# Block sums laid in one run, block products in another order, and down units split by adding DMAs in a two-layer encoder

## The chip, the cores and the metric

The kernel runs on one core of one Trainium2 chip. The metric is the device time of one execution in microseconds (us); the times given are medians of several runs. The engines are named as in the profile: PE is TensorE (matmuls), PEld its weight loads, DVE is VectorE, ACT is ScalarE, POOL is GpSimd, and SP is the engine that issues most of the DMAs.

## What is computed

The reference is an encoder of two layers on 512 frames of 1024 features, in float32. Each layer has a half-weighted feed-forward block (FFN), a mixer and another FFN:

```python
for layer in range(DEPTH):                       # DEPTH = 2
    h = _rmsnorm(x, ffn1_norm[layer])
    x = x + 0.5 * _swiglu(h, ffn1_w_gate[layer], ffn1_w_up[layer], ffn1_w_down[layer])
    h = _rmsnorm(x, mix_norm[layer])
    ...                                          # even: SSD and S5 mixers; odd: band attention and pooling
    x = x + mixed
    h = _rmsnorm(x, ffn2_norm[layer])
    x = x + 0.5 * _swiglu(h, ffn2_w_gate[layer], ffn2_w_up[layer], ffn2_w_down[layer])

def _swiglu(h, w_gate, w_up, w_down):            # 1024 -> 2816 -> 1024
    return (jax.nn.silu(h @ w_gate) * (h @ w_up)) @ w_down
```

The four FFNs hold most of the work: 3 x 1024 x 2816 weights each. They are numbered 0 to 3 (`f0` to `f3`); the even mixer lies between `f0` and `f1`, the odd one between `f2` and `f3`.

## The kernel before

**Products in three parts.** The kernel multiplies in `float32r`, a rounded form of float32. So that little precision is lost, each operand is split in a high part (a rounded copy) and a low part (what the copy left over), and each product is three matmuls: high x high, high x low, low x high (`mm3`, L596). A tile `whl` of [128, 2, 1024] holds both parts of 128 x 1024 weights, a tile `hg` of [128, 2, 512] both parts of an activation.

**Units.** Weights come in units of 128 x 1024 (512 KB). `load_raw` (L498) issues the load into a `raw` tile from SP. The feeder (`feed`, L508) then splits the unit in one of two ways. `split` (L565) has ScalarE write the rounded copy and VectorE subtract it from the raw weights. `split_dma` (L576) has ScalarE write the negative of the rounded copy into the low part, lets a DMA from POOL's queue add the weights to it from HBM, and has ScalarE write the high part: no VectorE, one more ScalarE copy and a second reading of the weights. `BY_DMA` (L52) says which units go which way: the key is the unit's name with, for `wgu` and `wdn`, the FFN's number; the range is over the unit's index (`by_dma`, L105). For `wdn` that index is the half of the output columns, `cg`, which is 0 or 1.

**FFN items.** `ffn_items` (L69) lists an FFN's work: 11 pairs of hidden tiles (q = 0 to 10), each with a gate (i = 0) and an up side (i = 1). The first q (eight in FFN 0, two in FFNs 1 to 3) are done in the plain way, four units `wgu` of 24 matmuls with 512 columns per q. The rest are "pairs". The down units (`wdn`, 22 in an FFN, 24 matmuls with 512 columns each) of a group of three q are put between the items of the next group, so that in the steady part a pair and a down unit take turns.

**Pairs.** A pair multiplies a 2 x 2 arrangement of weight blocks by a 2 x 2 arrangement of activation blocks with seven block products in place of eight. Sums of weight blocks (made by VectorE from two raw units, L541 to L551) and sums of activation blocks (`blocks`, L876, once per FFN) go into it. W1 and W2 are blocks of the weights themselves, W3 and W4 hold sums; N are the normed activations; TA and TB are lists of four `hg` tiles with sums, each of two sums of 256 columns. `block` (L904) is one block product of four steps: three matmuls of 256 columns in each, or, where it is `wide`, one of 512 columns (high weights by the high and the low part of a block sum at once) and one of 256. The parts of a block sum lie 512 elements apart, so that a wide matmul reads two runs of 256.

`pair` (L924) works in three PSUM banks X, Y and Z. In the order of the code before, with the names that are used below:

| block | line | what |
|---|---|---|
| X1 | L940 | W1 x N[0:4] into X; VectorE then makes p1 from it |
| Z4 | L944 | W4 x N[4:8] into one half of Z |
| (rest) | L946 | the last block of an earlier pair, where no down unit came between |
| Y3 | L949 | W3 x TA into Y, wide; `plus` then reads both halves of Y (two additions) |
| X1b | L951 | W1 x N[4:8], added to X |
| Z3 | L955 | W3 x TA into the other half of Z |
| Y4 | L962 | W4 x TB, wide, added to Y; `plus` reads Y again |
| Y2 | L969 | W2 x TB, wide, added to Y, after the next down unit |

An addition to a bank that VectorE has yet to read has to wait for that reading. Y2 takes its weights from the smaller tile `wh`, so its matmuls show as `ps<-hg,wh`; all other blocks and the down units show as `ps<-hg,whl`. Only q = 2, i = 1 of FFNs 1 to 3 has an earlier pair's rest in front of it (`before` in the code); the other 57 of 60 pairs do not.

**The order of the work** is written out by the program itself. `Clock` (L111) is a model of the engines and DMAs with a cost for each operation. At every few matmuls, `tick` (L285) lets the feeder and the waiting threads put in what the model holds to be ready (`on`, L320: the inputs are there, and the engine's queue is short enough). Threads stand in the order of `PRIO` (L58): a lower number goes first; among equal ones, a new thread goes in front, except `evac` (the reading of a plain unit's PSUM), which goes behind. While the FFN 0 runs, the thread `prep` prepares the S5 mixer with many small VectorE operations. All the program's instructions are issued through one helper, so that the profile gives L207 for them; groups are told apart by their tiles.

Of the kernel before, what the change touches and what calls it, by code (L numbers as in the profile page):

```python
# [14 lines left out]
PSUM = bass.MemoryType.PSUM  # L15
# [17 lines left out]
for _i, _pools in enumerate(((),(3,),(2,),(1,0))):  # L33
# [18 lines left out]
BY_DMA = {"wgu1": (1, 4), "wgu2": (1, 4), "wgu3": (1, 4), "wev": (13, 16), "wglu": (0, 2), "wevo": (0, 1), "wod": (8, 16), "wodo": (0, 1)}  # L52
# [5 lines left out]
PRIO = {"evac": 0, "gate": 0, "small": 5, "prep": 6, "blocks": 0, "s5_bounce": 1, "s5_quarter": 0, "s5_gate": 0, "s5_eighth": 1,  # L58
        "ssd_dt": 1, "conv": 1, "ssd_chunk": 1, "ssd_tail": 0, "z": 2, "qk_norm": 0, "pool": 3, "attn": 2}
LIVE = 3  # L60
CHAINS = 2
# [49 lines left out]
class Clock:  # L111


    def __init__(self):
        self.t = dict.fromkeys(list(ENGINES.values()) + ["RING", "DMA"], 0.0)
        self.t["ACT"], self.t["RING"], self.t["DVE"], self.t["PE"] = 1.9, 0.65, 0.6, 0.95
        self.w, self.r, self.floor, self.stuck = {}, {}, 0.0, 0
        self.lanes, self.born = [0.0] * 8, {}

    @property  # L120
# [24 lines left out]
    def cost(eng, op, out, kw):  # L145
# [12 lines left out]
        ptr = any(hasattr(kw.get(k), "space") for k in ("scalar", "scalar1"))  # L158
        return (0.128 if ptr else 0.068) + n / (1920 if one else 960) * (1 if eng == "DVE" else 2)

    def note(self, eng, op, args, kw):
        out = kw.get("out", args[0] if args else None)
        outs = [out] + ([kw["accum_out"]] if "accum_out" in kw else [])
        ins = [v for k, v in kw.items() if k not in ("out", "accum_out") and hasattr(v, "free_size")]
        dma = op == "dma_start"
        at = self.t["RING"] if dma else self.t[eng]
        for ap in ins:
            for b in self.blocks(ap):
                t, e = self.w.get(b, (0.0, ""))
                at = max(at, t + (0.15 if e != eng else 0.11 if eng != "PE" else 0.0))  # L170
        for ap in outs:
            at = max(at, self.born.get(ap.name, 0.0))
            for b in self.blocks(ap):
                t, e = self.w.get(b, (0.0, ""))
                at = max(at, 0.0 if dma and e == "DMA" else t if e == eng else t + 0.1, self.r.get(b, 0.0))
        if dma and eng == "POOL":
            self.t["POOL"] = max(at, self.t["POOL"]) + 1.1
            end = max(self.t["DMA"], self.t["POOL"] + 1.0) + max(0.18, out.free_size() * out.partition_size() * 4 / 360e3)
            self.t["DMA"] = end
            end += 0.95  # L180
        elif dma:
            at = max(at, self.lanes.pop(0))
            self.t["RING"] = at + 0.48
            end = max(self.t["DMA"], at + 1.1) + max(0.06, out.free_size() * out.partition_size() * 4 / 360e3)
            self.t["DMA"] = end
            end += 1.06
            self.lanes.append(end)
        else:
            end = at + self.cost(eng, op, out, kw)
            self.t[eng] = end  # L190
        for ap in outs:
            for b in self.blocks(ap):
                self.w[b] = (max(end, self.w.get(b, (0.0, ""))[0]), "DMA" if dma else eng)
        for ap in ins:
            for b in self.blocks(ap):
                self.r[b] = max(self.r.get(b, 0.0), end)
# [55 lines left out]
class Builder:  # L252
# [26 lines left out]

    def phase(self, name):  # L280
        self.name = name
        self.backlog, self.guard, self.most = BACKLOG[name], GUARD[name], AHEAD[name]


# [296 lines left out]

    def split_steps(self, src, dst, scale=None):
        nc = self.nc
        yield from self.on("ACT", src)
        if scale is None:
            nc.scalar.copy(out=dst[:, 0], in_=src)
        else:
            nc.scalar.activation(out=dst[:, 0], in_=src, func=AF.Copy, scale=scale)
        yield from self.on("DVE", dst[:, 0])
        if scale is None:  # L590
            nc.vector.tensor_tensor(out=dst[:, 1], in0=src, in1=dst[:, 0].bitcast(F32), op=ALU.subtract)
        else:
            nc.vector.scalar_tensor_tensor(out=dst[:, 1], in0=src, scalar=scale, in1=dst[:, 0].bitcast(F32),
                                           op0=ALU.mult, op1=ALU.subtract)
# [153 lines left out]
    def ffn(self, f, gi, then, prepare=None):  # L748
        nc, tc = self.nc, self.tc
        self.phase(f"f{f}")  # L750
        self.f, self.then, self.final, self.sideb = f, then, False, 2
        h = self.begin_norm(gi)
        with ExitStack() as st:
            self.ft = st.enter_context(tc.tile_pool(name=self.n("ft"), bufs=2))
            ex = ExitStack()
            prep = None
            if prepare is not None:
                prep = prepare(ex.enter_context(tc.tile_pool(name=self.n("prep"), bufs=1)))
# [11 lines left out]
            self.N, self.TA, self.TB = h, [], []  # L770
            grown, pending = False, None
            for key in ffn_items(f):
                if not grown and not self.running(prep) and CLASSIC[f == 0] < NFF // 2:
# [27 lines left out]
                elif key[0] == "pair":  # L801
                    q, i = key[2:]
                    if i == 0:
                        t = {}
                    last = self.pair(w, t, "us" if i else "gs", pending)

                    def pending(last=last, t=t, q=q, i=i):
                        last()
                        if i == 0:
                            nc.scalar.activation(out=t["gs"], in_=t["gs"], func=AF.Silu)  # L810
                        else:
                            self.add("gate", self.gate(t, g, q, [1] * 4, 1))
                            if q == NFF // 2 - 1:
                                self.give(*self.N, *self.TA, *self.TB)
                else:
                    cg, kp = key[2:]
                    grp = next(gr for gr in GROUPS if kp in gr)
                    if kp == grp[0]:
                        pss = [None] * 4
                        if cg == 0 and grp == GROUPS[-1]:  # L820
                            self.tail()
                    self.out_unit(pss, w, g, kp, cg, kp == grp[0], kp == grp[-1], 0.5, "a")
                    self.give(w)
                    if cg == 1:
                        self.give(g[2 * kp], g[2 * kp + 1])
                    if pending:
                        pending()
                        pending = None
# [47 lines left out]
    def blocks(self, h, gi, late):  # L876
# [5 lines left out]
        for kk in range(4):  # L882
# [11 lines left out]
            v.tensor_tensor(out=t4, in0=n2[:, a], in1=t2, op=ALU.subtract)  # L894
            self.give(tn)
            for c, d in ((lo, self.TA), (hi, self.TB)):
                t = yield from self.grab("hg")
                yield from self.split_steps(rt[:, c], t)
                d.append(t)
            self.give(rt)  # L900
        self.xhold, self.reserve = False, 0


    def block(self, ps, t, at, rhs, c, more=False, wide=False):  # L904
        nc = self.nc
        for kk in range(4):
            self.until(lambda: len(rhs) > kk)
            w = slice(at + kk * P, at + kk * P + P)
            r = rhs[kk]
            first, last = kk == 0 and not more, kk == 3  # L910
            o = ps[:, 0:256]
            go = dict(start=first, stop=False, skip_group_check=more)
            if wide:
                nc.tensor.matmul(out=ps.rearrange("p (a b) -> p a b", a=2), lhsT=t[:, 0, w], rhs=r[:, :, c], **go)
            else:
                nc.tensor.matmul(out=o, lhsT=t[:, 0, w], rhs=r[:, 0, c], **go)
                go["start"] = False
                nc.tensor.matmul(out=o, lhsT=t[:, 0, w], rhs=r[:, 1, c], **go)
            nc.tensor.matmul(out=o, lhsT=t[:, 1, w], rhs=r[:, 0, c], start=False, stop=last, skip_group_check=more)
            self.tick()  # L920


# [1 line left out]
    def pair(self, w, t, tag, before):  # L924
# [26 lines left out]
        self.block(X, W1, 512, N[4:8], lo, more=True)  # L951
        self.give(W1)
        times(dst[:, 0, lo], X[:, lo], lo)
        self.free(X)
# [12 lines left out]

        def last():
            self.block(Y, W2, 0, TB, hi, more=True, wide=wide)  # L969
            self.give(W2)  # L970
            plus(dst[:, 1, lo], Y, p1)
            self.free(Y)
# [1120 lines left out]
```

## Time and profile before

| | |
|---|---|
| runs before | 1817.4, 1820.8, 1824.5 us; median 1820.8 us |
| profiled execution, its own time | 1818.1 us |
| its span, first to last instruction | 1816.4 us |
| granted TensorE clock | 0.999 |
| FFN 0 with what lies beside it | 0 to 367 us: PE busy 360.7, DVE 311.4, ACT 129.7 |
| even mixer | 367 to 545 us: PE 169.2, DVE 150.4, ACT 93.6 |
| FFN 1 | 545 to 932 us: PE 384.5, DVE 326.3, ACT 156.0 |
| FFN 2 | 932 to 1282 us: PE 347.8, DVE 307.6, ACT 137.4 |
| odd mixer | 1282 to 1475 us: PE 192.7, DVE 130.4, ACT 107.7 |
| FFN 3 | 1475 to 1816 us: PE 335.3, DVE 292.6, ACT 122.0 |
| DMA queues | q1 (issued by SP): 196.5 MB; q0 (issued by POOL): 18.4 MB |

In a row that groups instructions stand: line, engine, operation, tiles (out<-in), shape and count; then busy time and the mean length of one in ns; then the engine's idle time just before them and what ended it. A row of waits reads "who waits <- for whom: us in total, times, longest". A row of the timeline has the start, the length from the first start to the last end, and what ran, with the idle time before it in brackets. Lengths of matmuls overlap, since one starts before the one ahead of it has ended: the distance of two starts tells what a matmul costs. A row by stages has the stretch and its length, busy us and number for PE, PEld, DVE, ACT and POOL, the granted clock, the DMA share and GB/s.

### The profile page before, as it was taken

What the parts mean: (1) busy time and instruction counts of PE and PEld (TensorE: products, weight loads), DVE (VectorE), ACT (ScalarE), POOL (GpSimd) and SP (SyncE); (2) the same over time, 40 slices, a digit from 0 to 9 for tenths busy, and PEclk for the clock granted to TensorE, in tenths of its full rate; (3) what the DMA queues carried; (4) which work ended last, traced back from release to release, by engine and by line L of the source; (5) the groups of instructions that cost most, each with busy time, mean ns of one, the idle gap of its engine ahead of it and who ended that gap; (6) DMA issues with size and microseconds to landing.
All of it is one profiled execution on the core that took longest, in us unless ns stands there. A gap on an engine that the chain in (4) does not pass through costs nothing.

```text
span 1816.4 us, 26183 instructions
## 1 busy us (share of the span) xinstructions
PE 1790.0 (99%) x10082; PEld 1535.7 (85%) x10082; DVE 1518.7 (84%) x2902; ACT 746.4 (41%) x1032; POOL 34.0 (2%) x53
## 2 busy tenths in 40 slices
PE   9999999999999999999999999999999999999999
PEld 7877888878778888888888898988888888988887
DVE  8999878777885899998779998987678679999984
ACT  4224433233584533333354333323466564333331
POOL 0000000000010000000010000000000010000000
PEclk9999999999999999999999999999999999999999
DMA  5256433336674532333343333333325452333331
GB/s 194 88 152 194 130 93 93 116 136 196 173 181 139 127 107 96 101 104 107 126 119 102 105 105 105 105 106 115 111 82 116 129 134 87 105 105 104 106 103 71
DMA packets 83341, 216.57 MB, mean 119 GB/s; under 512 B 18288, under 2 KB 30608, under 8 KB 82064
## 3 DMA queue, kind: packets, MB, share of 16 engines
q1 hardware_dynamic: 78032, 196.52, 33.7%
q0 software_dynamic: 5040, 18.35, 6.0%
q8 instruction: 79, 1.29, 0.3%
q14 instruction: 46, 0.38, 0.1%
q10 hardware_dynamic: 144, 0.02, 0.0%
HBM read 202.26 MB, written 12.60 MB: 118 GB/s over the span
## 4 chain that ended last, share of the span: by engine, by line
PE 64%; DVE 23%; DMA 6%; issue 4%; ACT 3%; SPq 0%; DVEq 0%; ACTq 0%
PE ps L207 64%; DVE whl L207 5%; DVE raw L207 4%; DVE us L207 4%; DMA raw<-in_wgu_dram 3%; ACT whl L207 2%; DVE gs L207 2%; DVE hg L207 2%; DVE x L207 1%; DVE wh L207 1%; DVE p L207 1%; DMA raw<-in_wev_dram 0%; DMA prm<-prm 0%; SPq L207 0%; DMA hg<-s5us 0%
## 5 line engine op out<-in xcount | busy, mean ns | idle before, releaser
L207 PE MATMUL ps<-hg,whl 128*128 128x512 f32 (+1 forms) x8400 | 1596.6, 349 | 12.4 <-DVE gs L207 6.1
L207 PEld LDWEIGHTS ps<-hg,whl 128*128 128x128 f32 x8400 | 1341.3, 189 | 221.4 <-DVE gs L207 10.8
L207 ACT CAST whl<-raw 128x1024 fp32r<-128x1024 f32 x374 | 391.1, 1048 | 500.9 <-PE ps L207 356.1
L207 DVE TENSOR_TENSOR whl<-raw,whl 128x1024 fp32r<-128x1024 f32 x339 | 412.2, 1219 | 100.6 <-ACT whl L207 100.3
L207 DVE TENSOR_TENSOR raw<-raw,raw 128x512 f32<-128x512 f32 (+1 forms) x212 | 129.5, 646 | 2.5
L207 ACT CAST hg<-us 128x512 fp32r<-128x512 f32 x88 | 52.0, 618 | 156.1 <-DVE us L207 155.9
L207 ACT ACTIVATE gs<-gs 128x1024 f32<-128x1024 f32 x44 | 46.6, 1060 | 159.9 <-DVE gs L207 159.9
L207 DVE SCALAR_TENSOR_TENSOR x<-ps,x 128x512 f32<-128x512 f32 x128 | 83.4, 683 | 19.3 <-PE ps L207 19.3
L207 PE MATMUL ps<-hg,wh 128*128 128x512 f32 x480 | 94.2, 339 | 0.9 <-DVE gs L207 0.9
L207 PEld LDWEIGHTS ps<-hg,wh 128*128 128x128 f32 x480 | 77.2, 188 | 13.8 <-DVE gs L207 1.6
L207 DVE TENSOR_TENSOR raw<-raw 128x512 f32<-128x512 f32 (+1 forms) x92 | 54.7, 595 | 19.0 <-DMA raw<-in_wgu_dram 18.4
L207 DVE TENSOR_TENSOR gs<-ps,gs 128x256 f32<-128x256 f32 x150 | 63.5, 424 | 4.1
L207 DVE TENSOR_TENSOR us<-ps,us 128x256 f32<-128x256 f32 x150 | 63.5, 423 | 4.1
L207 DVE TENSOR_TENSOR hg<-us,hg 128x512 fp32r<-128x512 f32 x88 | 59.2, 684 | 2.8 <-ACT hg L207 2.7
L207 DVE TENSOR_TENSOR us<-ps,p 128x256 f32<-128x256 f32 x90 | 37.8, 420 | 26.4 <-PE ps L207 26.2
L207 DVE TENSOR_TENSOR us<-gs,us 128x1024 f32<-128x1024 f32 x44 | 53.7, 1220 | 0.8
L207 DVE TENSOR_TENSOR p<-ps,rsB 128x256 f32<-128x256 f32 x120 | 49.9, 416 | 0.0
L207 ACT ACTIVATE hg<-x,gains 128x512 fp32r<-128x512 f32 x48 | 33.6, 720 | 31.2 <-DVE x L207 28.6
L207 DVE TENSOR_TENSOR gs<-ps,p 128x256 f32<-128x256 f32 x90 | 37.8, 420 | 8.7 <-PE ps L207 6.9
L207 DVE TENSOR_TENSOR us<-ps,rsB 128x512 f32<-128x512 f32 (+1 forms) x62 | 36.0, 581 | 6.3 <-PE ps L207 6.2
L207 DVE TENSOR_TENSOR wh<-raw,wh 128x512 fp32r<-128x512 f32 x60 | 41.0, 684 | 0.0
L207 DVE SCALAR_TENSOR_TENSOR hg<-x,gains,hg 128x512 fp32r<-128x512 f32 x48 | 35.5, 746 | 5.7 <-ACT hg L207 5.7
(258 smaller groups left out, 1083.4 us busy)
## 6 DMA issues: line engine op xcount, KB each, us to landing
raw<-in_wgu_dram SPq DMA_DIRECT2D x176, 512.0 KB, 3.5
raw<-in_wdn_dram SPq DMA_DIRECT2D x88, 512.0 KB, 4.1
whl<-in_wgu_dram POOLq DMA_DIRECT2D x18, 512.0 KB, 6.7
raw<-in_wev_dram SPq DMA_DIRECT2D x16, 512.0 KB, 4.1
prm<-prm SPq DMA_DIRECT2D x8, 1024.0 KB, 6.9
raw<-in_wod_dram SPq DMA_DIRECT2D x12, 512.0 KB, 3.5
raw<-in_wevo_dram SPq DMA_DIRECT2D x8, 512.0 KB, 6.9
raw<-in_wodo_dram SPq DMA_DIRECT2D x8, 512.0 KB, 6.6
```

The costliest lines, as they stand in the source:

```text
L207: r = f(*args, **kw)
```

## The change

It has five parts.

1. The block sums: the `hg` tile is filled as (c, j, b), c the sum (two), j the part (high, low), b its 256 columns. The two parts of one sum lie side by side, and a wide matmul reads one run of 512. ScalarE and VectorE write the tile through the same view.
2. `pair`: where no rest of an earlier pair stands in front, Z4 moves behind Y3. In all pairs Z3 moves in front of X1b, together with the operations on Z; `W3` is then given back before `W1`.
3. `BY_DMA`: all down units of FFNs 1 to 3 (3 x 22) are split by `split_dma`.
4. `PRIO`: `blocks` has priority 1 in place of 0.
5. `Clock`: in FFN 0 alone, a VectorE operation costs 0.09 us more in the model when its partition quarter differs from that of the operation before it that read or wrote the same memory, and a reciprocal costs 5 ns more per element.

```diff
+BY_DMA = {"wdn1": (0, 2), "wdn2": (0, 2), "wdn3": (0, 2), "wgu1": (1, 4), "wgu2": (1, 4), "wgu3": (1, 4), "wev": (13, 16), "wglu": (0, 2), "wevo": (0, 1), "wod": (8, 16), "wodo": (0, 1)}
...
+PRIO = {"evac": 0, "gate": 0, "small": 5, "prep": 6, "blocks": 1, "s5_bounce": 1, "s5_quarter": 0, "s5_gate": 0, "s5_eighth": 1,
...
+    def moved(self, ins, out):
+        at = lambda ap: (ap.space == PSUM, ap.start_partition() // 32)
+        held = any(self.reads.get(m, q) != q for m, q in map(at, ins))
+        m, q = at(out)
+        held = held or self.writes.get(m, q) != q
+        self.writes[m] = q
+        for m, q in map(at, ins[::-1]):
+            self.reads[m] = q
+        return 0.09 if held else 0.0
...
             end = at + self.cost(eng, op, out, kw)
+            if eng == "DVE" and self.fine:
+                end += self.moved([ap for ap in ins if ap.free_size() > 1], out)
+                if op == "reciprocal":
+                    end += out.free_size() * 0.005
...
     def phase(self, name):
         self.name = name
+        self.clk.fine = name == "f0"
...
     def split_steps(self, src, dst, scale=None):
         nc = self.nc
+        whole, dst = dst if isinstance(dst, tuple) else (dst[:, 0], dst)
...
-        yield from self.on("DVE", dst[:, 0])
+        yield from self.on("DVE", whole)
...
                 t = yield from self.grab("hg")
-                yield from self.split_steps(rt[:, c], t)
-                d.append(t)
+                tv = t.rearrange("p a b -> p (a b)").rearrange("p (c j b) -> p j c b", c=2, j=2)
+                yield from self.split_steps(rt[:, c].rearrange("p (c b) -> p c b", c=2), (t, tv))
+                d.append(tv)
+                self.TS.append(t)
...
-                nc.tensor.matmul(out=ps.rearrange("p (a b) -> p a b", a=2), lhsT=t[:, 0, w], rhs=r[:, :, c], **go)
+                nc.tensor.matmul(out=ps.rearrange("p (a b) -> p a b", a=2), lhsT=t[:, 0, w], rhs=rhs[kk][:, :, c], **go)
...
-        Z = self.main_ps()
-        self.block(Z[:, hi], W4, 512, N[4:8], hi)
         if before:
+            Z = self.main_ps()
+            self.block(Z[:, hi], W4, 512, N[4:8], hi)
             before()
         t[tag] = dst = self.ftile(tag)
         Y = self.main_ps()
-        self.block(Y, W3, 512, TA, hi, wide=wide)
+        self.block(Y, W3, 512, TA, 1, wide=wide)
         plus(dst[:, 0, hi], Y, p1)
+        if not before:
+            Z = self.main_ps()
+            self.block(Z[:, hi], W4, 512, N[4:8], hi)
+        self.block(Z, W3, 0, TA, 0)
+        self.give(W3)
+
+        add(dst[:, 0, hi], Z[:, lo], dst[:, 0, hi])
+        p5 = new("p5", 1)
+        times(p5, Z[:, hi], hi)
+        add(dst[:, 0, hi], dst[:, 0, hi], p5)
         self.block(X, W1, 512, N[4:8], lo, more=True)
         self.give(W1)
         times(dst[:, 0, lo], X[:, lo], lo)
         self.free(X)
-        self.block(Z, W3, 0, TA, lo)
-        self.give(W3)
-
-        add(dst[:, 0, hi], Z[:, lo], dst[:, 0, hi])
-        p5 = new("p5", 1)
-        times(p5, Z[:, hi], hi)
-        add(dst[:, 0, hi], dst[:, 0, hi], p5)
-        self.block(Y, W4, 0, TB, lo, more=True, wide=wide)
+        self.block(Y, W4, 0, TB, 0, more=True, wide=wide)
```

More of the change, by code (lines that the diff above doesn't have):

```diff
@@ L51 @@
 GUARD = {"f0": 2.5, "even": 1.5, "f1": 1.5, "f2": 1.5, "odd": 2.0, "f3": 1.5}
-BY_DMA = {"wgu1": (1, 4), "wgu2": (1, 4), "wgu3": (1, 4), "wev": (13, 16), "wglu": (0, 2), "wevo": (0, 1), "wod": (8, 16), "wodo": (0, 1)}
+BY_DMA = {"wdn1": (0, 2), "wdn2": (0, 2), "wdn3": (0, 2), "wgu1": (1, 4), "wgu2": (1, 4), "wgu3": (1, 4), "wev": (13, 16), "wglu": (0, 2), "wevo": (0, 1), "wod": (8, 16), "wodo": (0, 1)}
 LOADS = (1, 4)
@@ L57 @@
 PREP_SLACK = 4.0
-PRIO = {"evac": 0, "gate": 0, "small": 5, "prep": 6, "blocks": 0, "s5_bounce": 1, "s5_quarter": 0, "s5_gate": 0, "s5_eighth": 1,
+PRIO = {"evac": 0, "gate": 0, "small": 5, "prep": 6, "blocks": 1, "s5_bounce": 1, "s5_quarter": 0, "s5_gate": 0, "s5_eighth": 1,
         "ssd_dt": 1, "conv": 1, "ssd_chunk": 1, "ssd_tail": 0, "z": 2, "qk_norm": 0, "pool": 3, "attn": 2}
@@ L117, in __init__ @@
         self.w, self.r, self.floor, self.stuck = {}, {}, 0.0, 0
+        self.reads, self.writes, self.fine = {}, {}, True
         self.lanes, self.born = [0.0] * 8, {}
@@ L769, in ffn @@
             g, pss = [None] * NFF, None
-            self.N, self.TA, self.TB = h, [], []
+            self.N, self.TA, self.TB, self.TS = h, [], [], []
             grown, pending = False, None
@@ L813, in pending @@
                             if q == NFF // 2 - 1:
-                                self.give(*self.N, *self.TA, *self.TB)
+                                self.give(*self.N, *self.TS)
                 else:
@@ L905, in block @@
         nc = self.nc
+        o = ps[:, 0:256]
         for kk in range(4):
@@ L908, in block @@
             w = slice(at + kk * P, at + kk * P + P)
[L909 to L912, printed above, removed]
+            r = [rhs[kk][:, j, c] for j in range(2)]
+            go = dict(start=kk == 0 and not more, stop=False, skip_group_check=more)
             if wide:
-                nc.tensor.matmul(out=ps.rearrange("p (a b) -> p a b", a=2), lhsT=t[:, 0, w], rhs=r[:, :, c], **go)
+                nc.tensor.matmul(out=ps.rearrange("p (a b) -> p a b", a=2), lhsT=t[:, 0, w], rhs=rhs[kk][:, :, c], **go)
             else:
-                nc.tensor.matmul(out=o, lhsT=t[:, 0, w], rhs=r[:, 0, c], **go)
+                nc.tensor.matmul(out=o, lhsT=t[:, 0, w], rhs=r[0], **go)
                 go["start"] = False
-                nc.tensor.matmul(out=o, lhsT=t[:, 0, w], rhs=r[:, 1, c], **go)
-            nc.tensor.matmul(out=o, lhsT=t[:, 1, w], rhs=r[:, 0, c], start=False, stop=last, skip_group_check=more)
+                nc.tensor.matmul(out=o, lhsT=t[:, 0, w], rhs=r[1], **go)
+            nc.tensor.matmul(out=o, lhsT=t[:, 1, w], rhs=r[0], start=False, stop=kk == 3, skip_group_check=more)
             self.tick()
@@ L948, in pair @@
         Y = self.main_ps()
-        self.block(Y, W3, 512, TA, hi, wide=wide)
+        self.block(Y, W3, 512, TA, 1, wide=wide)
         plus(dst[:, 0, hi], Y, p1)
[L951 to L954, printed above, removed]
-        self.block(Z, W3, 0, TA, lo)
+        if not before:
+            Z = self.main_ps()
+            self.block(Z[:, hi], W4, 512, N[4:8], hi)
+        self.block(Z, W3, 0, TA, 0)
         self.give(W3)
@@ L961, in pair @@
         add(dst[:, 0, hi], dst[:, 0, hi], p5)
-        self.block(Y, W4, 0, TB, lo, more=True, wide=wide)
+        self.block(X, W1, 512, N[4:8], lo, more=True)
+        self.give(W1)
+        times(dst[:, 0, lo], X[:, lo], lo)
+        self.free(X)
+        self.block(Y, W4, 0, TB, 0, more=True, wide=wide)
         self.give(W4)
@@ L968, in last @@
         def last():
-            self.block(Y, W2, 0, TB, hi, more=True, wide=wide)
+            self.block(Y, W2, 0, TB, 1, more=True, wide=wide)
             self.give(W2)
```

## The prediction

> **What bounds the kernel now.** I read the page's head and its chain first, then the grouped waits of TensorE's weight loads stage by stage, then the timeline of TensorE through a few cycles of an FFN.
>
> ```profile
> span 1816.4 us, 26183 instructions
> PE 1790.0 (99%) x10082; PEld 1535.7 (85%) x10082; DVE 1518.7 (84%) x2902; ACT 746.4 (41%) x1032; POOL 34.0 (2%) x53
> PE 64%; DVE 23%; DMA 6%; issue 4%; ACT 3%; SPq 0%; DVEq 0%; ACTq 0%
> ```
>
> TensorE is hardly ever idle, so the time is the sum of its starts. Only two things can shorten it without taking matmuls away: a smaller step from one start to the next, and fewer waits. The steps, from two stretches of one shape each:
>
> ```profile
> 595.73 10.83 PE L207 MATMUL ps<-hg,whl 128*128 128x512 f32 x47
> 836.13 2.68 PE L207 MATMUL ps<-hg,whl 128*128 128x256 f32 x21
> L207 PE MATMUL ps<-hg,wh 128*128 128x512 f32 x240 | 87.3, 398 | 0.9 <-DVE gs L207 0.9
> L207 PE MATMUL ps<-whl,hg 128*128 128x512 f32 x96 | 22.5, 392 | 0.3 <-DVE rqv L207 0.3
> L207 PE MATMUL ps<-hg,whl 128*128 128x256 f32 x3360 | 489.7, 283 | 0.6 <-DVE p L207 0.6
> ```
>
> A 512-column matmul with one run of input takes (10.83 - 0.39) / 46 = 0.227 us, a 256-column one (2.68 - 0.28) / 20 = 0.120 us; 0.39 and 0.28 are the modelled lengths of the last one. The third row holds only two-run inputs (block sums), the fourth only one-run inputs: 398 against 392 ns.
>
> The cycle of an FFN in its steady part, TensorE alone. A row of `ps<-hg,wh` x8 is the last block product of a pair (the one from W2), so the distance between two such rows is one pair and one down unit:
>
> ```profile
> 788.30 1.56 PE L207 MATMUL ps<-hg,wh 128*128 128x512 f32 x8
> 789.70 14.19 PE L207 MATMUL ps<-hg,whl 128*128 128x256 f32 x88
> 803.73 1.56 PE L207 MATMUL ps<-hg,wh 128*128 128x512 f32 x8
> ...
> 834.73 1.56 PE L207 MATMUL ps<-hg,wh 128*128 128x512 f32 x8
> 836.13 7.33 PE L207 MATMUL ps<-hg,whl 128*128 128x256 f32 x56
> 844.48 7.13 PE L207 MATMUL ps<-hg,whl 128*128 128x512 f32 x32 [1.02 <-DVE gs L207]
> 851.45 1.56 PE L207 MATMUL ps<-hg,wh 128*128 128x512 f32 x8
> ```
>
> The undisturbed cycle takes 803.73 - 788.30 = 15.43 us, the other 851.45 - 834.73 = 16.72, or 1.29 more. Its 56 matmuls behind 836.13 are the blocks X1 (W1), Z4 (W4), Y3 (W3), X1 again and Z3 (12 + 12 + 8 + 12 + 12); the wait stands before the next one, **Y4** (W4 with TB), which adds to the bank that Y3 filled and so must let VectorE read that first. All such waits, by stage (545 to 932, 932 to 1282 and 1475 to 1816 us are FFNs 1 to 3 with little beside; the last two lines are of 0 to 367 us, FFN 0):
>
> ```profile
> PEld ps L207 <- DVE gs L207: 3.3, 6, 1.2
> PEld ps L207 <- DVE us L207: 0.7, 1, 0.7
> ...
> PEld ps L207 <- DVE gs L207: 3.0, 6, 0.9
> PEld ps L207 <- DVE us L207: 0.7, 1, 0.7
> ...
> PEld ps L207 <- DVE gs L207: 2.9, 6, 0.7
> PEld ps L207 <- DVE us L207: 0.7, 1, 0.7
> ...
> PEld ps L207 <- DVE gs L207: 3.2, 2, 2.6
> ...
> PEld ps L207 <- DVE p L207: 1.2, 2, 0.6
> ```
>
> That is 9.2 us on gs and 2.1 on us in FFNs 1 to 3: all that a better order there can win. One gs wait of each FFN is not at Y4 but at the first W2 block:
>
> ```profile
> L207 PEld LDWEIGHTS ps<-hg,wh 128*128 128x128 f32 x480 | 77.2, 188 | 13.8 <-DVE gs L207 1.6
> 646.20 4.56 PE L207 MATMUL ps<-hg,whl 128*128 128x512 f32 x32 [0.48 <-DVE us L207]
> ```
>
> So Y4 has 9.2 - 1.6 = 7.6 us on gs, and the us wait is at Y4 of q = 2, i = 1 (646.20 in FFN 1).
>
> **The change, part by part.**
>
> *Block sums in one run.* The wide matmuls (12 in each of 60 pairs, 720 in all) get one run of 512 in place of two of 256. No instruction is added: the ScalarE copy and the VectorE subtraction of a block sum keep their 512 elements and write two runs. By the rows, 398 - 392 = 6 ns each, 4.3 us together; by the cycle, 15.43 against 24 x 0.227 + 60 x 0.120 + 12 x 0.227 = 15.37, 5 ns each. But the mean could also hold the change from 512 to 256 columns and back, which stays. Bounds 0 and -4.3; I take **-3**, nearer to the direct rows. The page Advanced Engine Details and Errata of the Trainium skill (SBUF Cachelines) has an input slowed only where accesses leave a 16-byte line without a second hit, which two runs of 1 KB do not; by it this part is worth nothing.
>
> *Order in the pair.* Without an earlier pair's rest in front (57 of 60 pairs), X1, Z4, Y3, X1b, Z3, Y4 becomes X1, Y3, Z4, Z3, X1b, Y4. Between Y3 and Y4 stand three blocks in place of two: 36 narrow matmuls, 4.32 us for 2.88. What VectorE did before the wait of 844.48:
>
> ```profile
> 842.22 1.22 DVE L207 TENSOR_TENSOR us<-gs,us 128x1024 f32<-128x1024 f32 x1
> 843.54 0.42 DVE L207 TENSOR_TENSOR gs<-ps,p 128x256 f32<-128x256 f32 x1
> 844.00 0.42 DVE L207 TENSOR_TENSOR gs<-ps,gs 128x256 f32<-128x256 f32 x1
> ```
>
> The two reads of Y3 came behind a gate product, late by 844.48 - (836.13 + 52 x 0.120 + 4 x 0.227) = 1.2 us. The new 1.44 us covers that, the longest one, and so all 7.6 us; the us waits and the W2 waits stay, since q = 2, i = 1 has a rest in front and keeps its 2.88 us. X1b too now comes 4.27 us behind X1 (Y3 of 4 x 0.347 and two narrow blocks of 1.44) rather than 2.83, which covers the two waits on p in FFN 0 (1.2 us, longest 0.6). What is late next: the block sums and W3, needed 1.44 us earlier, while W4 is needed 1.39 later, and the gs tile of the pair, which is claimed 1.44 us sooner and waits for the gate product; both queue on VectorE only. Bounds 0 and -8.8; I take 0.9 of it, **-8**, since VectorE's queue is laid out anew and a few waits will come back.
>
> *Down units by DMA.* 66 units lose one VectorE subtraction each and get one ScalarE copy and one adding DMA of 512 KB from POOL's queue.
>
> ```profile
> L207 DVE TENSOR_TENSOR whl<-raw,whl 128x1024 fp32r<-128x1024 f32 x339 | 412.2, 1219 | 100.6 <-ACT whl L207 100.3
> 783.13 1.04 ACT L207 CAST whl<-raw 128x1024 fp32r<-128x1024 f32 x1
> whl<-in_wgu_dram POOLq DMA_DIRECT2D x18, 512.0 KB, 6.7
> DMA to landing us min/median/max: 5.3/7.1/9.6
> 656.00:932.00 276.00, 274.17 (x1627) 243.45 (x1627) 240.44 (x398) 102.56 (x121) 0.86 (x1) 1.00 0.34 109
> ```
>
> VectorE is freed of 66 x 1.22 = 80 us, ScalarE gets 66 x 1.05 = 69 us at a load of 102.56 / 276 = 37%. This is off the path as long as the product lands in time: the unit copied at 783.13 is used from 803.73 - 24 x 0.227 = 798.28, its low part 0.45 later, 15.6 us after the copy begins. The new way needs two copies' time at the most, 2.1, and 7.1 to land, 9.2 together, and 11.7 at the worst landing: 3.9 us of cover are left even then. If that cover is gone, each microsecond more costs up to 66. The freed VectorE time lies in a stage where it is busy 87%; it can shorten waits that the order has already taken, and some of the us waits. Bounds: -3.7 (all 2.1 and 1.6 left) and, from crowding, the rival below; I take **0**. On POOL's queue nothing stands behind these in an FFN; on ScalarE the next weight copy starts 1.05 us later, against the same 15 us.
>
> *Block sums at priority 1, and the dearer VectorE clock in FFN 0.* Both only move work in the written order. Priority 1 lets the readers of classic units go before the block sums; the nearest waits are the 0.7 us on us just behind that stretch. Gone or doubled in the three FFNs, they give the bounds -2.1 and +2.1; I take 0. In FFN 0 the model adds 0.09 us to VectorE operations that change partition quarter, so less preparation is pushed in front of evacuations; at stake are the 3.2 us on gs there (one of 2.6). Bounds -3.2 and +3 (the same again, elsewhere); I take **-1**.
>
> Sum: -3 - 8 - 1 = -12 us from the profiled execution's own 1818.1 (span 1816.4): **1806 us**. The runs before have the median 1820.8, 0.15% above it; I do not add that, and compare with the median for the chances.
>
> **The rivals.**
>
> *The wait only moves (1814 us).* For it: the waits are on VectorE's queue, not on Y3 itself, and the new order starts Y3 1.44 us earlier, in front of the same gate product and pair sums; if the planner packs that time with other work, Y4 waits as before. Against: the real distance grows by more than the longest wait, and VectorE loses 1.22 us per cycle. -3 and -1 are left: 1814.
>
> *The layout is worth nothing (1809 us).* The 6 ns are then the alternation of sizes. Against: 398 and 392 are lengths of the wide ones themselves, not of the steps behind them. -8 and -1 are left: 1809.
>
> *Slower: the adding DMAs crowd the raw loads (1839 us).* Place: the second raw load of each pair, behind which the four pair sums wait on VectorE.
>
> ```profile
> q0 software_dynamic: 298, 1.09, 54.9%
> q1 hardware_dynamic: 238, 0.91, 24.2%
> DMA to landing us min/median/max: 6.2/7.4/8.5
> 774.27 0.69 DVE L207 TENSOR_TENSOR raw<-raw 128x512 f32<-128x512 f32 x1 [2.53 <-DMA raw<-in_wgu_dram]
> 786.82 1.22 DVE L207 TENSOR_TENSOR whl<-raw,whl 128x1024 fp32r<-128x1024 f32 x1
> raw<-in_wgu_dram SPq DMA_DIRECT2D x176, 512.0 KB, 3.5
> ```
>
> Between 595 and 606 us three adding DMAs run, and raw loads land after 6.2 to 8.5 us in place of 3.5. By these shares an adding DMA of 0.52 MB holds the 16 engines 0.549 x 11 x 0.52 / 1.09 = 2.9 us, a plain one 1.5. VectorE already waits for such loads (2.53 us). W4 is ready at 788.04 and in the new order needed at 789.70 + 2.83 = 792.5: 4.5 us of cover. So it decides from a landing of 8 us; at 8.5 all 54 pairs of FFNs 1 to 3 lose 0.5 us, 27 together: 1818.1 + 27, less half of the forecast's 12, is 1839. Against: one adding DMA per 15.4 us raises the share from 0.34 to 0.34 + 2.9 / 15.4 = 0.53, not to the 0.79 of that stretch.
>
> The page SBUF — State Buffer of the Trainium skill (SBUF: two separate sides) has VectorE's double-port instructions lock POOL out while it writes descriptors, which would lengthen each landing; whether the 5.3 to 9.6 us above hold some of that, no row here can tell.
>
> **How the numbers follow.** Forecast 0.62, layout worth nothing 0.10, wait only moves 0.18, crowding 0.08, anything else 0.02. A half per cent of 1820.8, about what a measurement of this kernel tells from no change, is 9.1 us: faster means under 1811.7. The first case lies under it nearly whole, the second mostly, the third within: faster 0.70, same 0.22, slower 0.08. Low end: 1818.1 - 4.3 - 8.8 - 3.7 - 3.2 = 1798. High end: 1816, the third case with FFN 0 worse by 1 in place of better by 1; above it lie crowding and little else.
>
> **What would show it.** The 512-column rows on wh should fall to 392 to 394 ns. The gs waits of the weight loads in FFNs 1 to 3 should fall from 6 to 1 or 2 per FFN, the undisturbed cycle to 15.37 us, the p waits of FFN 0 to none. The VectorE row of 339 should read 273, with 84 adding DMAs in FFNs. I am wrong if Y4 waits stay above 4 us, if raw loads of wgu have a median above 5 us, or if a down unit's matmul waits for a DMA.

## The result and the profile after

| | before | after |
|---|---|---|
| median of 4 runs, us | 1820.9 (1817.4 to 1824.5) | 1837.2 (1835.4 to 1842.0) |
| ratio, 95% interval | | 1.0094 [1.0071, 1.0118] |
| the profiled execution, us | 1818.1 | 1836.3 |

The change makes the kernel slower by 16 us; the forecast was 1806 us, 31 us below. Head and chain of the changed kernel's page; its engines' instructions are recorded under L223, those of the kernel before under L207:

```profile
span 1834.6 us, 26387 instructions
PE 1793.4 (98%) x10082; PEld 1536.9 (84%) x10082; DVE 1448.1 (79%) x2836; ACT 808.8 (44%) x1098; POOL 90.1 (5%) x119
PE 58%; DVE 23%; DMA 11%; issue 4%; ACT 3%; SPq 1%; DVEq 0%; ACTq 0%
```

VectorE is busy 71 us less and the span is 18 us longer. In the chain the share of the DMAs went from 6% to 11%, that of TensorE from 64% to 58%. So something now waits for transfers. One of the costliest groups of the changed kernel (busy us, mean ns of one) and the largest of VectorE's grouped waits for a DMA (idle us, times, longest); the last fence is the same wait before:

```profile
L223 DVE TENSOR_TENSOR whl<-raw,whl 128x1024 fp32r<-128x1024 f32 x273 | 332.4, 1219 | 65.8 <-ACT whl L223 65.5
```

```profile
DVE raw L223 <- DMA raw<-in_wgu_dram: 65.9, 41, 4.8
```

```profile
DVE raw L207 <- DMA raw<-in_wgu_dram: 18.4, 23, 2.5
```

The subtractions fell from 339 to 273, as the change says. But the first sums of the pairs now wait 65.9 us together for their raw loads, 47.5 more than before. A wait on VectorE is no loss in itself. It became one on TensorE, as the waits of its weight loads in the three stages of FFNs 1 to 3 show (545 to 932, 932 to 1282 and 1475 to 1816 us):

```profile
PEld ps L223 <- DVE gs L223: 4.6, 5, 1.8
PEld ps L223 <- DVE us L223: 1.9, 2, 1.0
PEld ps L223 <- DVE p L223: 1.5, 2, 0.9
...
PEld ps L223 <- DVE gs L223: 4.7, 5, 1.8
PEld ps L223 <- DVE p L223: 2.2, 3, 1.0
PEld ps L223 <- DVE us L223: 1.9, 2, 1.0
...
PEld ps L223 <- DVE gs L223: 4.8, 5, 1.9
PEld ps L223 <- DVE us L223: 2.0, 2, 1.0
PEld ps L223 <- DVE p L223: 1.9, 3, 0.8
```

Together 25.5 us, where the kernel before had 9.2 + 2.1 = 11.3. That is 14.2 of the 18 us. Every one of these is a wait for VectorE to read PSUM; in these three stages TensorE has no wait for a weight at all. The timeline round the longest case gives the order of events (start, length, what, and in brackets the idle time before it):

```profile
802.11 0.86 POOL L223 DMA_DIRECT2D whl<-in_wdn_dram  x1 [13.97 <-ACT whl L223]
802.78 0.33 SPq L223 DMA_DIRECT2D raw<-in_wgu_dram  x1
...
807.38 7.33 PE L223 MATMUL ps<-hg,whl 128*128 128x256 f32 x56
809.27 0.69 DVE L223 TENSOR_TENSOR raw<-raw 128x512 f32<-128x512 f32 x1 [4.80 <-DMA raw<-in_wgu_dram]
...
812.93 1.22 DVE L223 TENSOR_TENSOR whl<-raw,whl 128x1024 fp32r<-128x1024 f32 x1
814.06 1.22 DVE L223 TENSOR_TENSOR us<-gs,us 128x1024 f32<-128x1024 f32 x1
...
815.38 0.42 DVE L223 TENSOR_TENSOR gs<-ps,p 128x256 f32<-128x256 f32 x1
...
816.32 7.12 PE L223 MATMUL ps<-hg,whl 128*128 128x512 f32 x32 [1.60 <-DVE gs L223]
```

ScalarE's two copies of a down unit release two things almost at once: the adding DMA on POOL's queue (802.11) and, since they free a raw buffer, the second raw load of the next pair (802.78). The load lands 6.5 us after its issue, at 809.24, which is 0.2 us behind the landing of the adding DMA (6.9 us after 802.11), and VectorE stands idle for 4.80 us in front of the sum that needs it. Behind the sum, in VectorE's order, come the other sums, a subtraction and a gate product, and only then (815.38) the reader of Y3's bank. TensorE has done its 56 matmuls by 814.7 and waits 1.60 us for that reader before Y4. In the window from 656 to 932 us, issue to landing of the raw loads (those of pairs and of down units together), before and after:

```profile
DMA to landing us min/median/max: 3.3/3.6/6.7
```

```profile
DMA to landing us min/median/max: 3.4/5.8/9.7
```

And the queues of the changed kernel from 660 to 930 us (packets, MB, share of 16 engines):

```profile
q1 hardware_dynamic: 8064, 29.36, 31.5%
q0 software_dynamic: 3024, 11.01, 24.2%
```

An adding DMA of 0.524 MB holds the 16 engines for 0.242 x 270 / (11.01 / 0.524) = 3.1 us, a plain load for 0.315 x 270 / (29.36 / 0.524) = 1.5 us.

### The profile page after: what moved, and what is told of

Its sections match the earlier page's. It is cut to its first block, busy times and chain, and to the rows that moved or that the text cites. A ratio compares the mean times of both kernels' runs of the same rounds, so it can differ in the third digit from the quotient of the medians.

```text
span 1834.6 us, 26387 instructions
## 1 busy us (share of the span) xinstructions
PE 1793.4 (98%) x10082; PEld 1536.9 (84%) x10082; DVE 1448.1 (79%) x2836; ACT 808.8 (44%) x1098; POOL 90.1 (5%) x119
## 4 chain that ended last, share of the span: by engine, by line
PE 58%; DVE 23%; DMA 11%; issue 4%; ACT 3%; SPq 1%; DVEq 0%; ACTq 0%
PE ps L223 58%; DMA raw<-in_wgu_dram 9%; DVE whl L223 5%; DVE raw L223 4%; DVE us L223 3%; ACT whl L223 3%; DVE hg L223 2%; DVE gs L223 2%; SPq L223 1%; DMA ssb<-acsd 1%; DVE ssb L223 1%; DVE p L223 1%; DVE s_t L223 1%; DVE ct L223 1%; DVE ex L223 1%
## 5 line engine op out<-in xcount | busy, mean ns | idle before, releaser
L223 PE MATMUL ps<-hg,whl 128*128 128x512 f32 (+1 forms) x8400 | 1598.5, 350 | 25.0 <-DVE gs L223 12.6
L223 PEld LDWEIGHTS ps<-hg,whl 128*128 128x128 f32 x8400 | 1342.2, 189 | 235.1 <-DVE gs L223 13.1
L223 ACT CAST whl<-raw 128x1024 fp32r<-128x1024 f32 x374 | 389.3, 1045 | 397.9 <-PE ps L223 255.1
L223 DVE TENSOR_TENSOR whl<-raw,whl 128x1024 fp32r<-128x1024 f32 x273 | 332.4, 1219 | 65.8 <-ACT whl L223 65.5
L223 ACT ACTIVATE whl<-raw 128x1024 fp32r<-128x1024 f32 x101 | 106.8, 1057 | 78.9 <-issue 52.2
L223 DVE TENSOR_TENSOR raw<-raw,raw 128x512 f32<-128x512 f32 (+1 forms) x212 | 130.6, 646 | 2.6
L223 ACT CAST hg<-us 128x512 fp32r<-128x512 f32 x88 | 51.5, 618 | 177.5 <-DVE us L223 177.4
L223 DVE SCALAR_TENSOR_TENSOR x<-ps,x 128x512 f32<-128x512 f32 x128 | 84.2, 684 | 32.1 <-PE ps L223 31.6
L223 DVE TENSOR_TENSOR raw<-raw 128x512 f32<-128x512 f32 (+1 forms) x92 | 54.8, 595 | 65.9 <-DMA raw<-in_wgu_dram 65.9
L223 POOL DMA_DIRECT2D whl<-in_wdn_dram x66 | 56.2, 852 | 873.5 <-ACT whl L223 688.7
L223 ACT ACTIVATE gs<-gs 128x1024 f32<-128x1024 f32 x44 | 46.6, 1060 | 113.3 <-DVE gs L223 113.3
L223 PE MATMUL ps<-hg,wh 128*128 128x512 f32 x480 | 94.3, 339 | 1.1 <-DVE gs L223 1.1
L223 PEld LDWEIGHTS ps<-hg,wh 128*128 128x128 f32 x480 | 77.3, 189 | 13.9 <-DVE gs L223 1.7
L223 DVE TENSOR_TENSOR us<-ps,us 128x256 f32<-128x256 f32 x150 | 63.6, 424 | 22.6 <-PE ps L223 17.6
L223 DVE TENSOR_TENSOR gs<-ps,gs 128x256 f32<-128x256 f32 x150 | 63.5, 423 | 5.7 <-PE ps L223 1.0
L223 DVE TENSOR_TENSOR us<-ps,p 128x256 f32<-128x256 f32 x90 | 37.9, 421 | 35.7 <-PE ps L223 35.6
L223 DVE TENSOR_TENSOR p<-ps,rsB 128x256 f32<-128x256 f32 x120 | 50.0, 417 | 18.9 <-PE ps L223 18.3
L223 DVE TENSOR_TENSOR hg<-us,hg 128x512 fp32r<-128x512 f32 x88 | 57.6, 684 | 2.7 <-ACT hg L223 2.7
L223 DVE TENSOR_TENSOR gs<-ps,p 128x256 f32<-128x256 f32 x90 | 37.8, 420 | 25.2 <-PE ps L223 23.8
L223 DVE TENSOR_TENSOR us<-gs,us 128x1024 f32<-128x1024 f32 x44 | 53.7, 1220 | 0.6
L223 ACT ACTIVATE hg<-x,gains 128x512 fp32r<-128x512 f32 x48 | 33.7, 719 | 34.4 <-DVE x L223 32.1
L223 DVE TENSOR_TENSOR wh<-raw,wh 128x512 fp32r<-128x512 f32 x60 | 41.0, 683 | 0.0
```

Of the source, the lines that this page charges most:

```text
L223: r = f(*args, **kw)
```

## The experiments

Ratios are to runs of the kernel before on the same chip, whose median was 1819.2 to 1820.0 us in the three sets.

**All but the down units, and the down units alone.** The first kernel is the changed one with the old BY_DMA, the second the kernel before with the new one.

```
-BY_DMA = {"wdn1": (0, 2), "wdn2": (0, 2), "wdn3": (0, 2), "wgu1": (1, 4), ...
+BY_DMA = {"wgu1": (1, 4), ...
```

> The kernel after, with its down units split by VectorE again; the other four parts of the change stay. Theory (the adding DMAs make the raw loads late, VectorE waits for them in its order, and the reads of PSUM behind come late): VectorE's wait for raw loads of wgu falls from 65.9 to about 18 us, the median landing of these loads from 4.1 to 3.5 us, the X1b and Y4 waits of FFNs 1 to 3 mostly go, time 1805 to 1814 us. Rival (the new order of the pair made the waits): the time stays near 1830 to 1837 us, with Y4 waits on gs of FFNs 1 to 3 above 9 us.

> The kernel before, with the down units of FFNs 1 to 3 split by adding DMAs and nothing else changed. Theory: raw waits of VectorE near 60 us, time 1840 to 1850 us, more than the whole change, since the shorter distance from Y3 to Y4 hides less. Rival (the order made the waits): 1815 to 1823 us.

Without the DMAs: 1809.0 us, 0.994 [0.9924, 0.9955]. The DMAs alone: 1837.4 us, 1.0095 [1.0078, 1.0112]. So the down units by DMA, with the order that the planner writes for them, are the whole loss: they cost 18 us on the kernel before, and 1837.2 - 1809.0 = 28 us on the rest of the change, whose gain they take with them. On the kernel before I had expected 1840 to 1850 us, more than the whole change, since the shorter distance from Y3 to Y4 would hide less; that isn't borne out. The three windows, VectorE's wait and the landing (656 to 932 us) without them:

```profile
PEld ps L223 <- DVE gs L223: 0.9, 2, 0.6
...
PEld ps L223 <- DVE gs L223: 0.6, 1, 0.6
PEld ps L223 <- DVE gs L223: 1.0, 2, 0.6
...
DVE raw L223 <- DMA raw<-in_wgu_dram: 19.3, 17, 2.6
...
DMA to landing us min/median/max: 3.3/3.6/5.3
```

The gs, us and p waits are 2.5 us in place of 25.5; the 23 us between account for most of the 28. The pair whose timeline stands above looks so without the DMAs:

```profile
802.56 1.23 DVE L223 TENSOR_TENSOR us<-gs,us 128x1024 f32<-128x1024 f32 x1
803.71 0.68 DVE L223 TENSOR_TENSOR raw<-raw 128x512 f32<-128x512 f32 x1
...
805.97 0.42 DVE L223 TENSOR_TENSOR gs<-ps,p 128x256 f32<-128x256 f32 x1
```

Here the gate product stands in front of the sums, the reader of Y3's bank (805.97) comes before the last of them, and VectorE does not wait for the load. So not only the landing differs but also VectorE's order. The time from issue to landing overstates how late the load is. Here the second raw load is issued at 799.22, 0.8 us before the W2 block of TensorE (800.04), and lands 2.7 us behind the start of that block; in the changed kernel it is issued 3.2 us before that block (805.98) and lands 3.3 us behind its start. Over the 45 steady pairs of the two traces the median load starts 2.2 us earlier in this cycle and lands 1.0 us later. With the DMAs alone:

```profile
DVE raw L207 <- DMA raw<-in_wgu_dram: 47.1, 36, 5.3
...
DMA to landing us min/median/max: 3.3/6.2/9.4
```

The late raw loads come with the DMAs, whatever else is changed.

**Order alone, then order and priority 1.** The kernel before with only the new sequence X1, Y3, Z4, Z3, X1b, Y4; then with "blocks" at 1 as well.

```
-"prep": 6, "blocks": 0, "s5_bounce": 1
+"prep": 6, "blocks": 1, "s5_bounce": 1
```

> The kernel before, with the new order of the pair's block products and nothing else changed. As predicted for this part: 8 us less, 1811 to 1815 us, with at most 2 gs waits per FFN in FFNs 1 to 3. Rival (the wait only moves): within 3 us of the kernel before, with new waits at the bank of Z4 for q = 2, i = 1.

> The kernel before with two parts of the change alone: the pair's order, and the block sums at priority 1. The order alone took the Y4 waits of the steady part away and put one gs wait of about 2.9 us per FFN into the first pairs; order, priority, layout and clock together took 0.994 of the kernel before. Theory (the order is worth something only with priority 1, which lets the first pairs' readers of PSUM go before the block sums): 0.994 to 0.996, with the big gs waits of the first pairs gone. Rival (the gain of the four parts together comes from the layout or the clock of FFN 0): 1.000 to 1.003, and the big waits stay.

The order alone: 1822.9 us, 1.0015 [1.0005, 1.0024], no gain at all. With priority 1: 1810.6 us, 0.9944 [0.9929, 0.9959]. The order alone clears the Y4 waits of the steady part but puts one of nearly 3 us into the first pairs of each FFN (545 to 932 us, the timeline there, and a row by stages of the 3.4 us behind the wait):

```profile
PEld ps L207 <- DVE gs L207: 3.1, 2, 2.7
```

```profile
652.26 0.68 DVE L207 TENSOR_TENSOR raw<-raw 128x512 f32<-128x512 f32 x1
652.98 1.90 DVE L207 TENSOR_TENSOR raw<-raw,raw 128x512 f32<-128x512 f32 x3
654.79 1.22 DVE L207 TENSOR_TENSOR whl<-raw,whl 128x1024 fp32r<-128x1024 f32 x1
655.93 1.22 DVE L207 TENSOR_TENSOR us<-gs,us 128x1024 f32<-128x1024 f32 x1
657.25 0.42 DVE L207 TENSOR_TENSOR gs<-ps,p 128x256 f32<-128x256 f32 x1
...
658.19 8.71 PE L207 MATMUL ps<-hg,whl 128*128 128x512 f32 x32 [2.47 <-DVE gs L207]
...
658.30:661.70 3.40, 3.40 (x11) 2.82 (x12) 3.37 (x6) 0.59 (x2) 0.00 (x0) 0.50 0.20 81
```

The reader of Y3's bank (657.25) stands behind four sums, a subtraction and a gate product, 5 us of work. The wait costs more than its own length: behind it the granted clock is 0.50 for 3.4 us, and Y4 with the down unit takes 8.71 us, where the same 32 matmuls took 7.13 in the kernel before (844.48). The trace has such a stretch behind each of these three waits (658, 1010 and 1542 us), and none in the pairs of FFNs 1 to 3 of the kernel before or of the one with priority 1. At 1.6 us each that is about 5 of the 12 us between 1822.9 and 1810.6. With priority 1 the same reader comes between the sums, and what is left in that window is

```profile
PEld ps L207 <- DVE gs L207: 0.6, 1, 0.6
```

So the two parts gain together what I gave to the order alone. What priority 1 does without the order wasn't tried.

**Layout alone, and layout with the clock of FFN 0.** The kernel before with the `tv` view of the block sums and nothing else; then also with `moved` and `fine` in the planner's model.

> The kernel before with the block sums' layout alone (both parts of each half side by side, so that the 512-column inputs have one run). Theory (the layout is worth nothing; the row of 398 ns stayed at 398 in the changed kernel, whose inputs have one run): 0.999 to 1.001, the rows on wh at 398 ns. Rival (the forecast's term of -3 us, hidden in the changed kernel by the lost time): 0.998 and rows of 392 to 394 ns.

> The kernel before with the layout and the dearer VectorE operations in the planner's model of FFN 0, nothing else. The forecast has -1 us for the clock; the kernel with all parts but the DMAs took 1.5 us less than the one with order and priority alone. Theory: 0.998 to 1.000, the gs wait of 2.6 us in FFN 0 gone. Rival (the clock moves the wait to other places of FFN 0, worth nothing): 0.9995 to 1.001.

Layout: 1819.4 us, 1.0003 [0.9994, 1.0011]. With the clock: 1819.0 us, 0.9996 [0.9987, 1.0005], the same within the error. The row that the forecast rested on, in the kernel with the new layout alone, by operation and shape:

```profile
L223 PE MATMUL ps<-hg,wh 128*128 128x512 f32 x240 | 87.3, 398 | 1.1 <-DVE gs L223 1.1
```

One run of input, and still 398 ns, the value of two runs. In FFN 0 the gs wait of 2.6 us is gone in the second kernel (the longest of the whole run is now 1.1), but waits for another VectorE result, bt, stand in its place: 3.4 us in three, the longest 1.6.

**The planner told of the slow DMA.** The changed kernel, whose planner holds that an adding DMA moves half as many bytes in a microsecond.

```
-... max(0.18, out.free_size() * out.partition_size() * 4 / 360e3)
+... max(0.18, out.free_size() * out.partition_size() * 4 / 180e3)
```

> The kernel after, with one figure of the written model changed: an adding DMA occupies the DMA engines for 2.9 us and not 1.45. Nothing on the chip gets less work; only the place of the instructions in the order changes. If the loss comes from pair sums that stand too early in VectorE's order, VectorE's raw waits fall under 40 us, and the time to 1810 to 1825 us. If late loads cost in themselves (the sums and so the weights come late, wherever they stand), the time stays at 1832 to 1840 us.

1834.0 us, 1.0077 [1.0057, 1.0097]: hardly anything. This was a poor test. In the written order the pair's raw loads stand ahead of the adding DMA, and the model lets transfers pass in that order; so a dearer adding DMA doesn't make the modelled load any later, and the sums stay nearly where they were.

**The planner told that the raw loads land late.** The changed kernel again, with no instruction added or removed; the model alone adds 1.6 us (then 3.0) to the landing of each 512 KB load in FFNs 1 to 3.

```
 def note(self, eng, op, args, kw):
...
             self.lanes.append(end)
+            if out.free_size() * out.partition_size() == 131072:
+                end += self.crowd
...
 def phase(self, name):
+        self.clk.crowd = 1.6 if name in ("f1", "f2", "f3") else 0.0
```

> The changed kernel, but the planner's model holds that a 512 KB weight load lands 1.6 us later in FFNs 1 to 3, which is about what the traces show under the adding DMAs; no instruction is added or left out, only the order on each engine differs. Theory (the loss is that VectorE's order places the four pair sums before their loads have landed, so reads of PSUM wait behind them): most of the 27 us over the same kernel without down units by DMA are recovered, to 0.995 to 1.002 of the kernel before, and VectorE's wait on raw falls from 65.9 to under 25 us. Rival (late loads cost in themselves, since the block products that need the sums come late, wherever the sums stand): 1.006 to 1.012, with TensorE's waits moved from gs to whl.

> As the changed kernel with its weight loads held to land later, 3.0 us in place of 1.6. The model then puts the pair sums another 2 to 3 us later; the weights of a pair had 2.8 to 8 us left between ready and use at 1.6. Theory (there is a broad best: VectorE's wait on raw goes on falling and most weights still come in time): 0.992 to 0.997. Rival (the sums now come late for the block products themselves): above 0.998, with TensorE waiting on whl in FFNs 1 to 3.

With 1.6 us: 1807.5 us, 0.9929 [0.9912, 0.9945]. All of the 28 us are back, with all 66 adding DMAs in place; that is more than the theory gave. Its VectorE wait, the landing (656 to 932 us), the gs wait of TensorE in the first window, and VectorE round the sums of the same pair as above:

```profile
DVE raw L225 <- DMA raw<-in_wgu_dram: 19.9, 14, 5.4
...
DMA to landing us min/median/max: 3.3/6.1/10.6
...
PEld ps L225 <- DVE gs L225: 0.2, 1, 0.2
...
802.15 1.23 DVE L225 TENSOR_TENSOR us<-gs,us 128x1024 f32<-128x1024 f32 x1
...
804.73 0.42 DVE L225 TENSOR_TENSOR gs<-ps,p 128x256 f32<-128x256 f32 x1
...
806.12 0.68 DVE L225 TENSOR_TENSOR raw<-raw 128x512 f32<-128x512 f32 x1
```

The loads are as late as in the changed kernel, 6.1 us. What changed is where the sums stand: the gate product and the reader of Y3's bank (804.73) now go ahead of them, and VectorE's wait is back at 19.9 us. So a late load costs nothing here, if nothing urgent is queued behind its first reader. With 3.0 us the kernel takes 1827.9 us, 1.0049 [1.0032, 1.0065]:

```profile
PEld ps L225 <- DMA whl<-in_wdn_dram: 21.7, 8, 5.2
```

VectorE hardly waits for raw any more (7.0 us), but now the down units themselves come too late, up to 5.2 us. The theory of a broad best is refuted. The rival's time came, but I had expected waits for the pair's weights; the chain of copies and loads moved back as a whole, and the down unit, with its adding DMA, was its tightest link.

**Half of the down units.** Every other one by DMA (`"wdn1": (0, 1)` and so on).

> The changed kernel with every other down unit of FFNs 1 to 3 (33 of 66) split by an adding DMA, the rest by VectorE. Theory (each adding DMA crowds the raw loads of the pair behind it, and the loss is paid pair by pair): half of the 27 us or somewhat less, 1.000 to 1.003, VectorE's wait on raw near 40 us. Rival (the loss comes from the whole plan of FFNs 1 to 3, not from single pairs): all or nothing of it, under 0.997 or over 1.006.

1830.1 us, 1.0060 [1.0045, 1.0076], so 21 of the 28 us with half of the DMAs. VectorE's wait on raw is 46.1 us, a little over half way from 19.3 to 65.9, as expected; the time isn't. Neither theory gives three quarters. The planner's order in this kernel is a third one, and I haven't found what it adds.

**Superfluous DMAs in an unchanged order.** The changed kernel without DMAs for down units, plus an adding DMA of 224 KB into a spare tile, of which the planner knows nothing: once released by the copy of the down unit, once by the next pair's first weight copy.

```
+    def extra_dma(self, t):
+        nc = self.tc.nc
+        nc.scalar.copy(out=self.dum[:, 0:1], in_=t[:, 0, 0:1].bitcast(F32))
+        nc.gpsimd.dma_start(out=self.dum, in_=self.due[:, 0:448], accum_op=ALU.add)
+        self.due = None
```

> The changed kernel with the down units split by VectorE as before, in the same written order, and beside it one superfluous adding DMA per down unit into a spare tile (224 KB, 44% of a down unit's, as much as there is room for), released by ScalarE's copy of the down unit, where the change's own DMA is released. Nobody reads the tile and the planner isn't told. Without the superfluous DMAs this kernel took 0.994. Theory (the transfer alone costs, by crowding the pair's raw loads, which are issued behind the same copy): 0.44 of the 27 us or somewhat less, 0.998 to 1.002, with raw loads of wgu above 3.5 us and more VectorE wait on raw. Rival (the loss comes from ScalarE's second copy or from the other order of the queues): 0.993 to 0.995.

> As the kernel with superfluous adding DMAs of 224 KB, but each is released by ScalarE's copy of the next pair's first weight, when that pair's raw loads have landed and the next ones are some 5 us off. Theory (what costs is the overlap with the pair's raw loads, not the traffic): 0.993 to 0.996, and VectorE's wait on raw near the 19 us of the kernel without them. Rival (the traffic costs wherever it stands): the same as where it is released by the down unit's copy.

At the down unit: 1814.9 us, 0.9967 [0.9957, 0.9977]. Later: 1811.7 us, 0.9952 [0.9936, 0.9969]. Landing (656 to 932 us) and VectorE's wait, first the one, then the other kernel:

```profile
DVE raw L223 <- DMA raw<-in_wgu_dram: 22.9, 19, 3.7
...
DMA to landing us min/median/max: 3.3/4.0/8.0
```

```profile
DVE raw L223 <- DMA raw<-in_wgu_dram: 18.7, 18, 2.5
...
DMA to landing us min/median/max: 3.3/3.7/5.6
```

The order of the real instructions is that of the kernel of 1809.0 us, so the slower landing (4.0 for 3.6) and the time, whose interval lies just above [0.9924, 0.9955], come from the transfers, with the one-column ScalarE copy of 0.19 us in front of each. Of the pairs' loads alone, the median rose only from 3.5 to 3.6 us; the rest of the 4.0 are loads of down units. It is 5 us, not the 12 of the theory: 44% of the bytes cost 18% of the time. Released later, landing and wait are almost those without any DMA, which fits the theory that overlap matters and not traffic. The times of these two kernels don't tell them apart, though: their intervals overlap, and the second issued only 45 of the 66 transfers, since some were replaced before a pair released them.

## Why the prediction was wrong

**Down units by DMA, forecast 0, measured +28 us.** This is the step that failed, and it failed in two places. First, I rejected the crowding of the raw loads because one adding DMA per cycle raises the mean share of the DMA engines only to 0.53. The mean came out nearly so, 0.242 + 0.315 = 0.56, but it doesn't bear on it: the adding DMA and the pair's second load are released by ScalarE's copies of the same down unit, 0.7 us apart in the cycle shown, so they overlap, and they land 0.2 us apart. The landing's median rose from 3.6 to 5.8 us, in part because the second load now starts earlier. Of my own marks for being wrong, waits before Y4 are far above 4 us (14.1 us on gs in the three stages, at most 1.7 of it at W2). The other, a median above 5 us for the raw loads of wgu, is met from 656 to 932 us (5.6), but not in the steady parts of FFNs 2 and 3 (4.9 in both) and not over the whole run (4.1): it was too coarse a sign, as it mixes loads with and without an adding DMA beside them. Second, I priced that rival through the cover of the weight W4 (4.5 us, so nothing before a landing of 8 us). In FFNs 1 to 3 of the changed kernel TensorE never waited for a weight. The path is VectorE's order: the sum that waits for the load has readers of PSUM behind it, and those have next to no cover. The rival's mechanism was right, its figure of 1839 came near the 1837 measured by luck, as it was worked out on another path and for a landing of 8.5 us.

What the runs show together: loads on time, in the order that the planner writes without the DMAs, 1809.0; loads late and the sums ahead of the gate product and the readers, 1837.2; loads late and the sums behind them, 1807.5. So late loads alone don't make the loss; the order has to put urgent work behind the sums. That this order would do no harm with loads on time is argued from VectorE's waits: no run has it. The planner set the order without knowing of the crowding.

**Order in the pair, forecast -8; block sums at priority 1, forecast 0.** Alone the order gave +3 (with some 5 us of it from the stretches at half the clock), together they gave 1810.6 - 1820.0 = -9.4 us. The size was nearly right, the attribution wrong: I gave the priority +-2.1 by the nearest wait and missed that the new order, which moves Y3 ahead, needs VectorE's readers of Y3 moved ahead too. Where they weren't, my rival "the wait only moves" came true, in the first pairs of each FFN.

**Layout, forecast -3, measured 0.** The row kept its 398 ns with one run of input, so the 6 ns come from something that the layout doesn't change; that it is the change from 512 to 256 columns and back, as I allowed, is not shown: it wasn't tried by itself, and the row of 392 ns is also of other tiles. An undisturbed cycle without the DMAs confirms it, 753.29 - 737.82 = 15.47 us, not 15.37:

```profile
737.82 1.56 PE L223 MATMUL ps<-hg,wh 128*128 128x512 f32 x8
...
753.29 1.56 PE L223 MATMUL ps<-hg,wh 128*128 128x512 f32 x8
```

The rule of the Trainium skill (Advanced Engine Details and Errata, SBUF Cachelines), by which two runs of 1 KB slow nothing, is the one that the measurement bears out.

**FFN 0, forecast -1.** With layout and clock 0.9996 [0.9987, 1.0005]: as forecast within the error, and not to be told from 0. The wait moved from gs to bt.

**The sum without the DMAs.** Forecast -12, measured 1809.0 - 1819.2 = -10.2 us. So four of five parts came near as a sum, but not one by one: the layout gave nothing of its -3, and the -8 of the order came only with the priority that I had put at 0. That the sum is so near is in part luck. The fifth part, at which I saw nothing to lose, turned it round.

**The rule of the Trainium skill on POOL's lock** (SBUF — State Buffer, SBUF: two separate sides) stays open: no run here varies VectorE's double-port work beside an adding DMA.

## What to carry to other kernels

Before you move work to a DMA that is cheap on average, look at what else the same event releases, and at what stands in order behind the first reader of that other transfer: the loss appears there, not at the moved work. A planner's order is only as good as its model of landings; when transfers get slower, tell it of the transfers that suffer, not only of the one that causes it. And an earlier start of a matmul group is worth something only if its readers move up as well.

## What the runs showed of the hardware

Adding DMAs from POOL's queue that take only 24.2% of the engines' time raised the median time from issue to landing of 512 KB loads by 60% (3.6 to 5.8 us, from 656 to 932 us); the one holds the engines for 3.1 us, the other for 1.5. In the cycle shown they are issued 0.7 us apart and land 0.2 us apart. That the overlap is the reason is not shown by itself: adding DMAs of 224 KB that were released later left a median of 3.7 us, but they were fewer.

In the kernel with the order alone, the granted clock was 0.50 for 3.4 us behind each of three waits of TensorE of 2.7 to 2.9 us, and the 32 matmuls there took 8.71 us in place of 7.13. Of the six longest waits of the kernel with 3.0 us, four have such a stretch beside them and two have none, so these runs give no rule.

A matmul of 512 columns has 398 ns in the profile among matmuls of 256 columns, whether its input is one run or two, where the row of 512-column matmuls of another tile has 392.
